# Compression layers of key and value as one set of 128-column products, and one transposition of the compressed probabilities per four heads

## The chip, the cores and the metric

The kernel runs on one core of one Trainium2 chip. The metric is device time in microseconds of one execution, lower is better. The core has five engines that run their own queues of instructions and wait for one another by semaphores: TensorE (PE; its weight loads are shown as PEld), VectorE (DVE), ScalarE (ACT), GpSimd (POOL) and SyncE (SP), which issues most of the DMAs.

## What is computed

Two layers of a decoder trunk on 256 tokens of width 1024: a recurrent block with its MLP, then native sparse attention with its MLP, and a final norm. The change lies in the attention layer. There each of four key/value groups has a compressed branch: blocks of 32 tokens (15 of them, 16 tokens apart) are flattened, a positional table is added, and a two-layer network with GELU makes one compressed key and one compressed value of each block.

```python
def _compress(z, pe, w1, w2):
    ...
    blocks = jnp.concatenate([chunks[:, r:r + nc] for r in range(CMP_RATIO)], axis=2)
    blocks = blocks + pe[None, None, :, None, :]
    flat = jnp.transpose(blocks, (0, 1, 3, 2, 4)).reshape(B, nc, G, CMP_LEN * DH)
    return jax.nn.gelu(flat @ w1, approximate=True) @ w2
...
        s_c = jnp.einsum('qghd,ngd->ghqn', qf, kc) - slopes * d_c.astype(jnp.float32)
        p_c = _masked_softmax(s_c, d_c >= 0)
        o_c = jnp.einsum('ghqn,ngd->qghd', p_c, vc)
...
        o = g[..., 0:1] * o_c + g[..., 1:2] * o_s + g[..., 2:3] * o_w
```

With 256 tokens there are only four blocks to select from, so all are selected, and the selected and the window branch are two causal attentions over 256 keys each, with keys and values of their own. The three branches are summed with sigmoid gates.

## The kernel before, in words

**Layout.** Activations are held transposed: 128 features on the partitions, 256 tokens along the row. Every large product is done in three matmuls on values split into a high and a low part (`mm3`, L307 to L310), because TensorE is fast on the split type; weights come by DMA into `raw`, ScalarE or VectorE make the high part (L316), VectorE the low one (L313). Smaller products are done in plain f32.

**Order.** The attention layer is one `Section`. Each step is added with the engines that may do it, an assumed duration, the keys it reads and writes and a wished time `t`; `Plan.emit` makes a list schedule of all steps from these and a seed, improves it by passes backwards and forwards, and issues every step in the order of the planned start. So a step that is dropped, added or given another duration may change the order of everything else on every engine, and which of ScalarE or VectorE does a step that either may do. The planner's numbers are no measured times.

**Compression.** `cproj` (L877) projects key and value for two groups each, four chunks in all; VectorE evicts each to one of three buffers `tt` (L881), and four copies, half of them by DMA (`move`, L823 to L826, on SyncE), lay its tokens into `zfs`, so that token offset and feature lie on the partitions (two offsets 16 apart times 64 features) and the block along the row: 60 blocks of four groups and two columns for the positional table, `ZW` = 62. `hidden` (L890) multiplies them with the first layer: for each of 16 offsets one product for key, whose 64 outputs go to the lower half of the partitions of PSUM bank 4, and one for value into the upper half. The 62 columns of the moving operand are followed by the GELU for both (L901 to L904). `kc_out` makes compressed keys (L908). `vc_out` first repeats the hidden values four times (`hv`), so that the product of L927 gives, for the four heads of a group that share them, 16 blocks each on 64 partitions; one product for each of four sets `a` of four heads, and VectorE multiplies each with a mask (L930) so that `bd[:, a]` is block-diagonal: four heads on 64 partitions, each with its own 64 output columns. The upper 64 partitions of `bd` and of the probabilities `pcs` are set to zero by GpSimd (L812, L814), since the product that uses them runs over 128 partitions.

**Attention.** `compressed(a)` (L985) does four heads at once: eight score products into bank 7 (L998), a softmax in eleven steps on VectorE (L1008 to L1020, one step of them on ScalarE), which leaves `cq`, 128 queries on the partitions and (half of the queries, head, block) along the row; two transpositions, one per half of the queries (L1035), into 64 partitions of bank 7, and an eviction to `pcs[a % 2]` by ScalarE (L1037). The heads' other two branches go through `scores` (L1058, L1059, with maximum on VectorE, L1065, and exponential on ScalarE, L1068), `rescale` (VectorE L1088 or ScalarE L1087), and `transposes` (L1099). `pv(j)` (L1104) then sums two heads' three branches in bank 7: first the compressed one (L1110, from `pcs` and `bd`, 256 queries at once), then the other two from `pT` and `vv`. Two heads' outputs go to the two halves of the partitions. Bank 7 is used by all of these in turn, and also by `vc_out`. Between these steps TensorE does the remaining query and key projections and, from the middle on, the first half of the output projection.

Of the kernel before, what the change touches and what calls it, by code (L numbers as in the profile page):

```python
# [68 lines left out]
EXTRA = [("gate", i) for i in range(4)] + [("w1k", 0), ("w1v", 0)]  # L69
# [150 lines left out]
def trunk_kernel(ctx: ExitStack, tc: tile.TileContext, x_in, vec_in, const_in, w2_in, wts, out):  # L220
# [557 lines left out]
    with ExitStack() as ph:  # L778
# [9 lines left out]
        bd = at.tile([P, 4, 4, 64], F32, name="bd")  # L788
# [16 lines left out]
        pcs = many([P, S], F32, "pc", 2)  # L805
# [58 lines left out]
        zfs = [zv(ptt, i * ZW * 16) for i in range(2)]  # L864
        zpt = [("pt", i, qc, b) for i in range(NPT) for qc in range(2) for b in range(2)]
        cb = pre.tile([P, 2], F32, name="cb")
        hid = pre.tile([P, 4, NCP], F32, name="hid")
        hv = pre.tile([P, 4, 2, 2, NCP], F32, name="hv")[64:]
# [21 lines left out]
        def hidden(b, t):  # L890
            hp = zview("hp", b, lambda x: x[:, :ZW])
            keys = [("zf", i, g, j) for i in range(2) for g in range(4) for j in range(2)]
            keys += [("zf", i, x) for i in range(2) for x in "pz"]
            for q_ in range(4):
                def run(e, q_=q_):
                    for l in range(4 * q_, 4 * q_ + 4):
                        for i in range(2):
                            e.matmul(hp()[own_(i)], w1[i][:, l * 64:(l + 1) * 64], zfs[i][:, :, l], start=l == 0, stop=l == 15)
                add("pe", 0.86, run, r=[("w1", i) for i in range(2)] + keys + zpt, w=[("ps", b)], t=t + 0.9 * q_)
            t += 3.6  # L900
            add("dve", 0.07, lambda e: e.tensor_copy(cb, hp()[:, 60:62]), r=[("ps", b)], w=["cb"], t=t)  # L901
            add("act", 0.2, lambda e: e.activation(hid[:, :, :NB], hp()[:, :60].rearrange("p (g n) -> p g n", g=4),
                                                   AF.Gelu_apprx_tanh, bias=cb[:, 0:1]),
                r=[("ps", b), "cb", "tab"], w=["hid"], t=t)  # L904

        def kc_out(t):
            o = zview("kco", 6, lambda x: x[:, :4 * NCP])
            add("pe", 0.3, lambda e: e.matmul(o(), w2raw[:64], hid[:64].rearrange("p g n -> p (g n)"), start=True, stop=True),  # L908
                r=["hid"], w=[("ps", 6)], t=t)
            o4 = lambda: o().rearrange("p (g n) -> p g n", g=4)  # L910
            add("act", 0.1, lambda e: e.copy(kc[:, :, 0], o4()), r=[("ps", 6), "kc0"], w=["kch"], t=t)
            for hf in range(2):
                own = own_(hf)
                add("dve", 0.15, lambda e, own=own, hf=hf: e.tensor_tensor(
                    kc[own, hf::2, 1], o4()[own, hf::2], kc[own, hf::2, 0].bitcast(F32), op=OP.subtract),
                    r=[("ps", 6), "kch", "kc0"], w=[("kcl", hf)], t=t)

        def vc_out(t):
            for g in range(4):
                dst = hv[:, g // 2 * 2:g // 2 * 2 + 2, :, g % 2].rearrange("p a b n -> p (a b) n")  # L920
                add([("act", 0.2, 0.0), ("dve", 0.15, 0.0)], copy(dst, hvs[:, g, None, :].to_broadcast([64, 4, NCP])),
                    r=["hid"], w=[("hv", g)], t=t)
            o = zview("vco", 7, lambda x: x[:64, :4 * 64].rearrange("p (a e) -> p a e", a=4))

            def run(e):
                for a in range(4):
                    e.matmul(o()[:, a], hv[:, a].rearrange("p b f n -> p (b f n)"), w2raw[64:, :64], start=True, stop=True)  # L927
            add("pe", 0.9, run, r=[("hv", g) for g in range(4)], w=[("ps", 7)], t=t)
            for a in range(4):
                add("dve", 0.34, lambda e, a=a: e.tensor_tensor(  # L930
                    bd[:64, a], o()[:, a, None, :].to_broadcast([64, 4, 64]),
                    cst[:64, C_BM:C_BM + 4, None].to_broadcast([64, 4, 64]), op=OP.mult), r=[("ps", 7)], w=[("bd", a)], t=t)
# [52 lines left out]
        def compressed(a, t, dt):  # L985
# [45 lines left out]
            ct_ = zview(("ct", a), 7, lambda x: x[:64, :S])  # L1031

            def tr(e):
                for qc in range(2):
                    e.transpose(ct_()[:, qc * P:(qc + 1) * P], sq_[:, qc].rearrange("p j n -> p (j n)"), identf)  # L1035
# [68 lines left out]
        def pv(j, t):  # L1104
# [4 lines left out]
            def run(e):  # L1109
                two = lambda c0, w, y, **k: [e.matmul(o()[own_(hf), c0:], w(hf), y(hf), **k) for hf in range(2)]  # L1110
                two(0, lambda hf: bd[:, a, j % 2 * 2 + hf], lambda hf: pcs[a % 2], start=True, stop=False)
# [4 lines left out]
            add("pe", 1.92, run, r=[("pT", n0 + i) for i in range(4)] + [("bd", a), "bd0", ("pc", a % 2), ("pc0", a % 2)] +  # L1116
# [95 lines left out]
def _arrange(inp):  # L1212
# [28 lines left out]
    w1 = {"w1k": f["nsa_w1_k"][0], "w1v": f["nsa_w1_v"][0]}  # L1241

    def piece(name, i):
# [16 lines left out]
        if name in w1:  # L1260
            w = w1[name].reshape(2, 16, 64, 64)
            return w.transpose(0, 2, 1, 3).reshape(P, -1)
# [21 lines left out]
    bm = np.where(np.arange(P)[:, None] // NCP % 4 == np.arange(8)[None, :], 1.0, 0.0)  # L1284
# [28 lines left out]
```

## Time and profile before

| what | value |
|---|---|
| median of 3 runs | 579.18 us (578.52 to 579.38) |
| the profiled execution | 579.59 us |
| its span, first to last instruction | 577.8 us |
| mean granted clock of TensorE | 0.994 |
| hidden layer's products on TensorE (L898) | 280.61 to 285.0 us |
| first compressed scores (L998) | 309.5 us |
| last weighted sum (L1110) | ends at about 383.1 us |

In the profile, times are in microseconds from the first instruction. A row of the timeline gives start, length, engine, line, operation, what is written from what, the shape of the written or loaded tile, and after an x how many equal ones follow each other. Matmuls are pipelined, so a row of several is as long as from the first start to the last end, and the step between two starts is the price of one. In brackets stands the idle time ahead and what ended it.

### The profile page before, as it was taken

The numbers are of one execution on the slowest core, as the hardware profiler recorded it, in microseconds if no ns is written. First come the engines' busy times: TensorE is split into PE (matmuls) and PEld (weight loads), VectorE is DVE, ScalarE is ACT, GpSimd is POOL, SyncE is SP. The second block draws the span as 40 slices with busy tenths as digits, with TensorE's granted clock in tenths as the row PEclk, the third lists the DMA queues.
The fourth block names the chain that finished last, engine by engine and source line by source line (L and its number), as shares of the span: only waits on it lengthen the run. The fifth ranks groups of instructions, "written<-read, shape, count | busy, mean of one in ns | idle before, by whom it ended". The sixth has DMA issues, their size and how long they took to land.

```text
span 577.8 us, 12305 instructions
## 1 busy us (share of the span) xinstructions
PE 566.2 (98%) x4878; PEld 554.0 (96%) x4878; DVE 409.5 (71%) x840; ACT 337.7 (58%) x655; POOL 46.8 (8%) x59
## 2 busy tenths in 40 slices
PE   8999999999999999999999999999999999999994
PEld 7999999999999999999999888999999999999993
DVE  6999998667765654656759999979676775553522
ACT  7699575755663533535447988865766564443400
POOL 1210000000000211312000000000000000222310
PEclk9999999999999999999999999999999999999997
DMA  8934666655656565566673253234655666466302
GB/s 296 387 120 142 206 216 204 214 184 195 203 187 219 180 201 204 177 200 242 188 246 115 70 160 101 89 110 138 199 200 195 187 199 236 152 213 219 111 1 73
DMA packets 32377, 103.66 MB, mean 179 GB/s; under 512 B 4016, under 2 KB 7216, under 8 KB 32320
## 3 DMA queue, kind: packets, MB, share of 16 engines
q1 hardware_dynamic: 31712, 102.29, 53.4%
q8 instruction: 38, 0.62, 0.4%
q10 hardware_dynamic: 576, 0.53, 0.3%
q14 instruction: 19, 0.16, 0.1%
q0 software_dynamic: 32, 0.07, 0.0%
HBM read 99.23 MB, written 1.05 MB: 174 GB/s over the span
## 4 chain that ended last, share of the span: by engine, by line
PE 85%; DVE 8%; DMA 4%; ACT 2%; issue 1%; SPq 0%; DVEq 0%
PE bank L308 25%; PE bank L309 25%; PE bank L310 25%; PE bank L1110 3%; PE bank L1099 2%; DVE wlo L313 2%; DVE xb L628 2%; DMA pt<-tt 1%; PE bank L1058 1%; DMA raw<-in_dram 1%; DMA xt<-in_dram 1%; PE bank L1059 1%; ACT whi L316 1%; PE bank L948 1%; PE bank L949 1%
## 5 line engine op out<-in xcount | busy, mean ns | idle before, releaser
L308 PE MATMUL bank<-hhl,whi 128*128 128x256 f32 x768 | 214.7, 280 | 1.2 <-DVE whi L316 1.2
L310 PE MATMUL bank<-hhl,wlo 128*128 128x256 f32 x768 | 212.6, 277 | 0.5 <-DVE wlo L313 0.5
L309 PE MATMUL bank<-hhl,whi 128*128 128x256 f32 x768 | 212.6, 277 | 0.1
L308 PEld LDWEIGHTS bank<-hhl,whi 128*128 128x128 f32 x768 | 144.2, 188 | 1.8 <-ACT x L545 1.3
L277 DVE TENSOR_TENSOR wlo<-raw,whi 128x1024 fp32r<-128x1024 f32 x115 | 143.7, 1270 | 2.3 <-ACT whi L268 2.3
L310 PEld LDWEIGHTS bank<-hhl,wlo 128*128 128x128 f32 x768 | 144.2, 188 | 0.9 <-DVE wlo L313 0.9
L309 PEld LDWEIGHTS bank<-hhl,whi 128*128 128x128 f32 x768 | 144.3, 188 | 0.6 <-DVE hhl L541 0.3
L308 PE MATMUL bank<-uhl,whi 128*128 128x256 f32 x512 | 141.5, 276 | 0.0
L309 PE MATMUL bank<-uhl,whi 128*128 128x256 f32 x512 | 141.4, 276 | 0.0
L310 PE MATMUL bank<-uhl,wlo 128*128 128x256 f32 x512 | 141.4, 276 | 0.0
L268 ACT CAST whi<-raw 128x1024 fp32r<-128x1024 f32 x116 | 118.0, 1039 | 23.1 <-issue 18.8
L308 PEld LDWEIGHTS bank<-uhl,whi 128*128 128x128 f32 x512 | 96.1, 188 | 0.0
L309 PEld LDWEIGHTS bank<-uhl,whi 128*128 128x128 f32 x512 | 96.1, 188 | 0.0
L310 PEld LDWEIGHTS bank<-uhl,wlo 128*128 128x128 f32 x512 | 96.1, 188 | 0.0
L313 DVE TENSOR_TENSOR wlo<-raw,whi 128x1024 fp32r<-128x1024 f32 (+2 forms) x74 | 79.4, 1094 | 6.8 <-ACT whi L316 6.6
L491 DVE TENSOR_TENSOR xt<-xt,bank 128x256 f32<-128x256 f32 x40 | 16.3, 418 | 86.4 <-PE bank L310 86.3
L316 ACT CAST whi<-raw 128x1024 fp32r<-128x1024 f32 (+2 forms) x64 | 61.3, 968 | 19.9 <-PE bank L309 5.4
L743 ACT ACTIVATE u<-t 128x256 f32<-128x256 f32 x64 | 26.7, 417 | 59.7 <-DVE t L738 58.7
L738 DVE SCALAR_TENSOR_TENSOR t<-bank,rstd 128x256 f32<-128x256 f32 x64 | 27.0, 424 | 46.8 <-PE bank L310 46.8
L1193 ACT ACTIVATE xg<-xt,vec 128x256 f32<-128x256 f32 x8 | 4.1, 511 | 48.0 <-DVE xt L491 48.0
L1068 ACT ACTIVATE pt<-pt,mx 128x128 f32<-128x128 f32 (+1 forms) x64 | 28.6, 448 | 4.2 <-DVE mx L1065 4.0
L461 POOL TENSOR_TENSOR acc<-xt 128x256 f32<-128x256 f32 x2 | 3.1, 1526 | 345.4 <-DVE xt L491 345.4
(182 smaller groups left out, 745.8 us busy)
## 6 DMA issues: line engine op xcount, KB each, us to landing
raw<-in_dram SPq DMA_DIRECT2D x173, 512.0 KB, 3.7
raw<-in_dram SPq DMA_DIRECT2D x4, 560.0 KB, 4.1
gw<-in_dram SPq DMA_DIRECT2D x4, 512.0 KB, 8.5
raw<-in_dram SPq DMA_DIRECT2D x6, 256.0 KB, 5.6
xt<-in_dram SPq DMA_DIRECT2D x4, 256.0 KB, 5.3
w<-in_dram SPq DMA_DIRECT2D x2, 512.0 KB, 5.5
kh<-kh SPq DMA_DIRECT2D x8, 64.0 KB, 2.8
kl<-tl SPq DMA_DIRECT2D x8, 64.0 KB, 2.5
```

The lines of the kernel that those rows point to most:

```text
L268: (act.copy if eng is None else eng.tensor_copy)(hi_t[i % NSPL][:, :n], raw_t[i % NRAW][:, :n])
L277: (eng or dve).tensor_tensor(lo[:, :n], raw_t[i % NRAW][:, :n], hi[:, :n].bitcast(F32), op=OP.subtract)
L308: pe.matmul(ps, wh, xh, start=start, stop=False)
L309: pe.matmul(ps, wh, xl, start=False, stop=False)
L310: pe.matmul(ps, wl, xh, start=False, stop=stop)
L313: return lambda e: e.tensor_tensor(o, a, h.bitcast(F32), op=OP.subtract)
L316: return lambda e: (e.copy if e is act else e.tensor_copy)(o, a)
L491: dve.tensor_tensor(xt[:, m], xt[:, m], z, op=OP.add)
L738: dve.scalar_tensor_tensor(t, z, 0.0, rs, op0=OP.max, op1=OP.mult)
L743: act.activation(u, t, AF.Square)
L1068: add("act", (0.39, 0.49)[qc], lambda e, row=row, j=j: e.activation(row, row, AF.Exp, bias=mx[:, j:j + 1], scale=-1.0, accum_out=sm[:, j:j ...
L1110: two = lambda c0, w, y, **k: [e.matmul(o()[own_(hf), c0:], w(hf), y(hf), **k) for hf in range(2)]
```

## The change

- **Hidden layer.** The first-layer weights of key and value are stored side by side on the host, so that one weight holds 128 columns: 64 for key, 64 for value. One product per offset, 16 instead of 32, multiplies it with the columns of both key and value (124). It yields four quarters, of which two are used: key's weights with key's columns, and value's with value's. The two DMA pieces `w1` keep their size, but the first now holds offsets 0 to 7 of both and the second offsets 8 to 15. Bias copy and GELU become two steps each, of 64 partitions.
- **Compressed values.** `hv` is laid out so that two products of 128 columns, one for each half `p` of the groups, replace four of 64; `bd` becomes 128 partitions with eight (half of the queries, head) of 64 columns; two masks of 512 columns replace four of 256.
- **Probabilities.** `cq` is transposed once, as 128x128, with (half of the queries, head, block) on the partitions, and evicted as 128x128 by ScalarE or VectorE. In `pv` each half of the queries then has its own block-diagonal columns: two products of 128 columns per head instead of one of 256.
- **No more zeros.** The three memsets on GpSimd go.

```diff
-EXTRA = [("gate", i) for i in range(4)] + [("w1k", 0), ("w1v", 0)]
+EXTRA = [("gate", i) for i in range(4)] + [("w1", 0), ("w1", 1)]
...
-        bd = at.tile([P, 4, 4, 64], F32, name="bd")
+        bd = at.tile([P, 2, 8, 64], F32, name="bd")
...
-        add("pool", 0.9, lambda e: e.memset(bd[64:], 0.0), w=["bd0"], t=-8)
-        for i in range(2):
-            add("pool", 0.3, lambda e, i=i: e.memset(pcs[i][64:], 0.0), w=[("pc0", i)], t=-8)
...
                     for l in range(4 * q_, 4 * q_ + 4):
-                        for i in range(2):
-                            e.matmul(hp()[own_(i)], w1[i][:, l * 64:(l + 1) * 64], zfs[i][:, :, l], start=l == 0, stop=l == 15)
-                add("pe", 0.86, run, r=[("w1", i) for i in range(2)] + keys + zpt, w=[("ps", b)], t=t + 0.9 * q_)
+                        e.matmul(hp(), w1[l // 8][:, l % 8 * P:(l % 8 + 1) * P], zall[:, :, l], start=l == 0, stop=l == 15)
+                add("pe", 0.89, run, r=[("w1", i) for i in range(2)] + keys + zpt, w=[("ps", b)], t=t + 0.9 * q_)
...
-                for a in range(4):
-                    e.matmul(o()[:, a], hv[:, a].rearrange("p b f n -> p (b f n)"), w2raw[64:, :64], start=True, stop=True)
-            add("pe", 0.9, run, r=[("hv", g) for g in range(4)], w=[("ps", 7)], t=t)
-            for a in range(4):
-                add("dve", 0.34, lambda e, a=a: e.tensor_tensor(
...
+                for p in range(2):
+                    e.matmul(o()[:, p], hv[:, p].rearrange("p b f n -> p (b f n)"), w2raw[64:, :64], start=True, stop=True)
+            add("pe", 0.45, run, r=[("hv", g) for g in range(4)], w=[("ps", 7)], t=t)
+            for p in range(2):
+                add("dve", 0.6, lambda e, p=p: e.tensor_tensor(
...
-                for qc in range(2):
-                    e.transpose(ct_()[:, qc * P:(qc + 1) * P], sq_[:, qc].rearrange("p j n -> p (j n)"), identf)
-            add("pe", 0.22, tr, r=[qk], w=b7, t=t)
-            add("act", 0.26, lambda e: e.copy(pc[:64], ct_()), r=b7, w=[pk], t=t)
+            add("pe", 0.11, lambda e: e.transpose(ct_(), sq_.rearrange("p q j n -> p (q j n)"), identf), r=[qk], w=b7, t=t)
+            add([("act", 0.3, 0.0), ("dve", 0.2, 0.15)], lambda e: copy(pc, ct_())(e), r=b7, w=[pk], t=t)
...
-                two(0, lambda hf: bd[:, a, j % 2 * 2 + hf], lambda hf: pcs[a % 2], start=True, stop=False)
+                for qc in range(2):
+                    cut = o()[:, qc * P:(qc + 1) * P]
+                    for hf in range(2):
+                        e.matmul(cut[own_(hf)], bd[:, p, qc * 4 + j % 2 * 2 + hf], pcs[a % 2], start=qc == 0, stop=False)
```

The new steps also give the planner other durations, so the order changes from the hidden layer on. Three places on TensorE matter below. The line numbers of the changed kernel are a little lower (L895 is the old L898, L1032 the old L1035, L1054 the old L1058, L1095 the old L1099).

First the hidden layer (`pt` holds the laid-out columns, `w` the weights), the value projection behind it (L948 to L950), key's output (L908) and value's (L927). Before:

```order
L310 MATMUL bank_3445<-hhl,wlo_92 128x256
L898 MATMUL bank_3477<-pt,w_3240 64x62
L898 MATMUL bank_3477<-pt,w_3241 64x62
...
L948 MATMUL bank_3522<-whi_86,hhl 128x304
...
L908 MATMUL bank_3543<-hid,w2raw 128x64
L927 MATMUL bank_3545<-w2raw,hv 64x64 x4
L948 MATMUL bank_3554<-whi_86,hhl 128x304
```

and now:

```order
L310 MATMUL bank_3434<-hhl,wlo_92 128x256
L895 MATMUL bank_3472<-pt,w_3240 128x124 x8
L895 MATMUL bank_3472<-pt,w_3241 128x124 x8
L948 MATMUL bank_3501<-whi_86,hhl 128x304
...
L908 MATMUL bank_3524<-hid,w2raw 128x64
L948 MATMUL bank_3528<-whi_86,hhl 128x304
...
L927 MATMUL bank_3538<-w2raw,hv 128x64 x2
L948 MATMUL bank_3528<-whi_86,hhl 128x304
```

The 32 products have become 16. Twelve value products stand between the hidden layer and key's output as before; value's output, which followed at once, now comes six value products later.

Second, the first scores: `sa_3213` and `sb_3217` hold the first query chunk, `sa_3214` the second. Before:

```order
L1059 MATMUL bank_3766<-kl,sb_3217 128x256
L308 MATMUL bank_3731<-hhl,whi_85 128x256
...
L1058 MATMUL bank_3781<-kh,sb_3217 128x512
L1059 MATMUL bank_3781<-kl,sb_3217 128x512
L1058 MATMUL bank_3788<-kh,sa_3214 128x256
```

and now:

```order
L1055 MATMUL bank_3744<-kl,sb_3217 128x256
L308 MATMUL bank_3710<-hhl,whi_85 128x256
...
L308 MATMUL bank_3758<-hhl,whi_86 128x256
...
L1054 MATMUL bank_3769<-kh,sb_3217 128x512
L1055 MATMUL bank_3769<-kl,sb_3217 128x512
L1054 MATMUL bank_3775<-kh,sa_3214 128x256
```

Six products stood ahead of the 512-column scores; now there are twelve, the last six of another projection.

Third, from the last compressed score of the first four heads (L998) to their transposition (`cst,cq`). Before:

```order
L998 MATMUL bank_3796<-kc,sb_3218 128x32 x2
L308 MATMUL bank_3811<-hhl,whi_86 128x256
...
L1099 MATMUL bank_3833<-cst,pt 128x128 x3
L1099 MATMUL bank_3840<-cst,pt 128x128 x3
L1058 MATMUL bank_3846<-kh,sb_3218 128x512
...
L1058 MATMUL bank_3864<-kh,sb_3218 128x256
...
L1099 MATMUL bank_3879<-cst,pt 128x128 x3
L1099 MATMUL bank_3885<-cst,pt 128x128 x3
L308 MATMUL bank_3893<-hhl,whi_87 128x256
...
L1035 MATMUL bank_3914<-cst,cq_3260 64x128 x2
```

and now:

```order
L998 MATMUL bank_3785<-kc,sb_3218 128x32 x2
L308 MATMUL bank_3758<-hhl,whi_86 128x256
...
L1054 MATMUL bank_3810<-kh,sb_3218 128x256
L1055 MATMUL bank_3810<-kl,sb_3218 128x256
L1095 MATMUL bank_3816<-cst,pt 128x128 x3
L1095 MATMUL bank_3822<-cst,pt 128x128 x3
...
L308 MATMUL bank_3850<-hhl,whi_87 128x256
...
L1095 MATMUL bank_3862<-cst,pt 128x128 x3
L1095 MATMUL bank_3868<-cst,pt 128x128 x3
L1032 MATMUL bank_3876<-cst,cq_3260 128x128
```

Before, 36 products (L308 to L310), 12 transpositions, two 512-column and two 256-column score products stood between them. Now it is 24 products, 12 transpositions and the two of 256 columns; the two 512-column ones and 12 products come after the transposition. On VectorE the same stretch, from L1008 to L1020, has 12 rows of other heads' work among its own ten instead of 14. Over the whole section five of the rescaling steps (L1088) go from VectorE to ScalarE, and one of the four evictions of `pcs` goes to VectorE.

On SyncE the eight DMAs of the compression (`pt<-tt`) stand in the same order behind the same loads as before.

More of the change, by code (lines that the diff above doesn't have):

```diff
@@ L804, in trunk_kernel @@
         w1 = many([P, 1024], F32, "w1", 2)
-        pcs = many([P, S], F32, "pc", 2)
+        pcs = many([P, P], F32, "pc", 2)
         for i in range(2):
@@ L896, in run @@
                     for l in range(4 * q_, 4 * q_ + 4):
-                        for i in range(2):
-                            e.matmul(hp()[own_(i)], w1[i][:, l * 64:(l + 1) * 64], zfs[i][:, :, l], start=l == 0, stop=l == 15)
-                add("pe", 0.86, run, r=[("w1", i) for i in range(2)] + keys + zpt, w=[("ps", b)], t=t + 0.9 * q_)
+                        e.matmul(hp(), w1[l // 8][:, l % 8 * P:(l % 8 + 1) * P], zall[:, :, l], start=l == 0, stop=l == 15)
+                add("pe", 0.89, run, r=[("w1", i) for i in range(2)] + keys + zpt, w=[("ps", b)], t=t + 0.9 * q_)
             t += 3.6
[L901 to L904, printed above, removed]
+            for i in range(2):
+                own, c = own_(i), i * ZW
+                add("dve", 0.1, lambda e, own=own, c=c: e.tensor_copy(cb[own], hp()[own, c + 60:c + 62]), r=[("ps", b)],
+                    w=[("cb", i)], t=t)
+                add("act", 0.25, lambda e, own=own, c=c: e.activation(
+                    hid[own, :, :NB], hp()[own, c:c + 60].rearrange("p (g n) -> p g n", g=4), AF.Gelu_apprx_tanh,
+                    bias=cb[own, 0:1]), r=[("ps", b), ("cb", i), "hid", "tab"], w=[("hid", i)], t=t)
         def kc_out(t):
@@ L1115, in run @@
                     two(P, lambda hf: vv[:, 1, b, 2 * p + hf], lambda hf: y(hf)[:, S:], start=False, stop=b == 1)
-            add("pe", 1.92, run, r=[("pT", n0 + i) for i in range(4)] + [("bd", a), "bd0", ("pc", a % 2), ("pc0", a % 2)] +
+            add("pe", 1.92, run, r=[("pT", n0 + i) for i in range(4)] + [("bd", p), ("pc", a % 2)] +
                 [("v", h, b) for h in range(2) for b in range(2)], w=bk, t=t)
@@ L1240, in _arrange @@
     wo = wo[perm]
-    w1 = {"w1k": f["nsa_w1_k"][0], "w1v": f["nsa_w1_v"][0]}
+    w1 = [f["nsa_w1_%s" % n][0].reshape(2, 16, 64, 64).transpose(0, 2, 1, 3).reshape(P, 16, 64) for n in "kv"]
+    w1 = np.concatenate(w1, axis=2)
     def piece(name, i):
@@ L1259, in piece @@
             return wv[2 * i:2 * i + 2].transpose(1, 0, 2).reshape(P, -1)
-        if name in w1:
-            w = w1[name].reshape(2, 16, 64, 64)
-            return w.transpose(0, 2, 1, 3).reshape(P, -1)
+        if name == "w1":
+            return w1[:, i * 8:i * 8 + 8].reshape(P, -1)
         if name == "q":
@@ L1283, in _arrange @@
         mc.append(np.where(ok, 1.0, 0.0))
-    bm = np.where(np.arange(P)[:, None] // NCP % 4 == np.arange(8)[None, :], 1.0, 0.0)
+    bm = np.where(np.arange(P)[:, None] // NCP == np.arange(8)[None, :], 1.0, 0.0)
     qs = np.zeros((P, 8))
```

20 lines of the change are left out of this document (10 added, 10 removed).

## The prediction

> **What bounds the kernel now.** I read the page first, then TensorE's waits, then the busy time by stretch over the attention section (263 to 402 us), then the timeline where the change lies. The page:
>
> ```profile
> span 577.8 us, 12305 instructions
> PE 566.2 (98%) x4878; PEld 554.0 (96%) x4878; DVE 409.5 (71%) x840; ACT 337.7 (58%) x655; POOL 46.8 (8%) x59
> ```
>
> TensorE is busy throughout. That holds in the changed section too, where VectorE comes close behind it (two of the stretches; the columns are the stretch, its length, then PE, PEld, DVE, ACT, POOL):
>
> ```profile
> 310.00:320.00 10.00, 10.00 (x88) 9.13 (x89) 9.58 (x48) 9.35 (x32) 0.00 (x0) 1.00 0.07 16
> 350.00:360.00 10.00, 10.00 (x88) 8.10 (x87) 9.77 (x41) 9.04 (x31) 0.00 (x0) 1.00 0.17 33
> ```
>
> Of TensorE's waits, two lie in this section, both on short copies by DMA:
>
> ```profile
> PE bank L898 <- DMA pt<-tt: 0.3, 1, 0.3
> PE bank L1058 <- DMA sa<-tl: 0.2, 1, 0.2
> ```
>
> So a microsecond is gained or lost here only where TensorE's own steps get shorter or longer, or where its new order meets a wait. Memsets taken off GpSimd, evictions by ScalarE or VectorE, and their smaller counterparts cost nothing by themselves, while TensorE has other products to do.
>
> **Hidden layer.** TensorE's timeline around it, and, from the groups by line, L898 itself and the one f32 product with a full 128-column weight and many repeats (L648):
>
> ```profile
> 280.40 0.28 PE L310 MATMUL bank<-hhl,wlo 128*128 128x256 f32 x1
> 280.61 0.41 PE L898 MATMUL bank<-pt,w 128*64 128x62 f32 x2
> 281.37 3.65 PE L898 MATMUL bank<-pt,w 128*64 128x62 f32 x62 [0.35 <-DMA pt<-tt]
> 284.94 0.41 PE L948 MATMUL bank<-whi,hhl 128*128 128x304 f32 x1
> 285.19 0.30 PE L949 MATMUL bank<-wlo,hhl 128*128 128x304 f32 x1
> 285.33 0.30 PE L950 MATMUL bank<-whi,hhl 128*128 128x304 f32 x1
> L898 PE MATMUL bank<-pt,w 128*64 128x62 f32 x64 | 4.1, 287 | 0.3 <-DMA pt<-tt 0.3
> L648 PE MATMUL bank<-xb,gw 128*128 128x256 f32 x64 | 14.1, 379 | 0.0
> ```
>
> The code has 32 products of 64 columns; the chip shows 64, each f32 product being two instructions. From 281.37 to 284.94 there are 62: 0.058 us each, 0.115 per pair of halves. The change leaves 32 instructions with 124 moving columns. L648 takes 14.1 / 64 = 0.22 us for 256 columns; half of it is 0.11. So 32 x 0.11 = 3.5 us instead of 64 x 0.058 = 3.7, from the same DMA on: the last one starts at 281.37 + 31 x 0.11 = 284.78. What is really saved is the passage into the next product. The last L898 starts at 281.37 + 3.65 - 0.29 = 284.73; L948 comes 0.21 after it and L949 0.25 after L948, where the step is otherwise 0.14 (285.19 to 285.33). A full-width f32 group should leave as the transposition of the next part does: 0.23 from its last instruction to the second product after it, here 0.03 more for the 304 columns. L949 comes at about 285.04 instead of 285.19: **-0.15 us** (between -0.3 and, if each instruction cost a whole 0.22, +3.5).
>
> The Trainium skill's "TensorEngine Tiling (Array Packing)", Theoretical Speedup, gives column tiles of up to 64 columns up to twice the throughput, which speaks against this change: the two old halves would run at once. Its "TensorE: Matmul & The Clock Gate", LDWEIGHTS (loading the stationary operand), prices a weight load by its columns, P / 1.2 ns, which makes an estimated 53 ns for 64 and 107 for 128, hence no difference; the trace's 0.058 per half agrees with this second rule, not the first. By the first alone the sum would be an estimated 1.7 us worse.
>
> **Transposition.** Two old ones at the first four heads, with the products around them, and three ordinary transpositions after:
>
> ```profile
> 316.39 0.28 PE L309 MATMUL bank<-hhl,whi 128*128 128x256 f32 x1
> 316.50 0.28 PE L310 MATMUL bank<-hhl,wlo 128*128 128x256 f32 x1
> 316.62 0.38 PE L1035 MATMUL bank<-cst,cq 128*64 128x128 f32 x2
> 316.76 0.37 PE L308 MATMUL bank<-hhl,whi 128*128 128x256 f32 x1
> 316.96 0.29 PE L309 MATMUL bank<-hhl,whi 128*128 128x256 f32 x1
> 317.56 0.49 PE L1099 MATMUL bank<-cst,pt 128*128 128x128 f32 x3
> ```
>
> The second L1035 starts at 316.62 + 0.11 = 316.73 (two end after 0.38, three of L1099 after 0.49: one more adds 0.11), 0.23 before L309. From L310 at 316.50 to L309 at 316.96 pass 0.46 us, in which L310 and L308 are 2 x 0.115 (316.39 to 316.50 is 0.11): the pair costs 0.23. A full-width one costs no more than a 64-column one by the same 0.11, so one goes away at each of four places. 4 x 0.11: **-0.43 us**, all on the path. The eviction of 128x128 instead of 64x256 lies beside products.
>
> **Weighted sums.** One of the eight groups of probabilities times values:
>
> ```profile
> 357.19 0.65 PE L1110 MATMUL bank<-pc,bd 128*64 128x256 f32 x4
> 357.68 1.47 PE L1110 MATMUL bank<-pT,vv 128*64 128x256 f32 x16
> 359.08 0.51 PE L1058 MATMUL bank<-kh,sa 128*128 128x512 f32 x1
> ```
>
> The four bd instructions, two pairs, take 0.49 until 357.68, of which I count 0.05 as entry: 0.22 a pair. The 16 that follow are four pairs of 256 and four of 128 columns; of the 1.40 until 359.08, 0.88 are the long ones and about 0.1 the exit, so a short pair takes about 0.11. The change makes four short pairs of two long ones: 0.44 either way. I add 0.01 for each of eight groups: **+0.1 us** (0 to +0.2).
>
> **Outputs of the compression.**
>
> ```profile
> 286.46 0.28 PE L950 MATMUL bank<-whi,hhl 128*128 128x256 f32 x1
> 286.74 0.43 PE L908 MATMUL bank<-hid,w2raw 64*128 64x64 f32 x2
> 287.98 0.30 PE L949 MATMUL bank<-wlo,hhl 128*128 128x304 f32 x1
> ```
>
> From 286.46 to 287.98 pass 1.52 us, of which about 0.26 are two products: the visit costs 1.26. Four f32 products become two of double width, but a new entry and exit come in, since six value products now stand between key's and value's output. An entry was at most 0.16 (286.46 to 286.74, less 0.12); an exit like the one after the hidden layer's some 0.2. I take **0** (-0.3 to +0.3). The Trainium skill, "TensorEngine Tiling (Array Packing)", Key Properties, says that a change of tiling mode drains TensorE; by it the hidden layer loses two drains and this place gains one. The 0.21 before L898 and L948 agree.
>
> **The new order.** Two waits move. First, the scores of the second query chunk:
>
> ```profile
> 308.15 0.40 PE L1059 MATMUL bank<-kl,sb 128*128 128x512 f32 x1
> 308.71 0.36 PE L1058 MATMUL bank<-kh,sa 128*128 128x256 f32 x1 [0.16 <-DMA sa<-tl]
> 309.25 0.40 PE L1059 MATMUL bank<-kl,sa 128*128 128x512 f32 x1
> 309.49 0.29 PE L998 MATMUL bank<-kc,sa 128*128 128x32 f32 x2
> ```
>
> A 512-column step is 0.24 (309.25 to 309.49); here it is 0.56. TensorE lost 0.32 us until the copy landed. The new order puts 12 products ahead instead of 6, and 6 x 0.115 = 0.69 covers that: **-0.3 us** (0 to -0.32). What is late next is the second point: TensorE may now come to the first compressed transposition too soon.
>
> ```profile
> 310.07 0.37 PE L998 MATMUL bank<-kc,sb 128*128 128x32 f32 x2
> L1008 DVE TENSOR_TENSOR cs<-bank,cst x4: 284/288/291, 311.0 to 362.1; 128x128 f32<-128x128 f32 x4
> L1020 DVE TENSOR_TENSOR cq<-cs,cm x4: 286/292/293, 315.4 to 366.4; 128x128 f32<-128x128 f32 x4
> L1065 DVE CUSTOM_DVE_ANT_0 pt<-bank,cst 128x256 f32<-128x256 f32 x32 | 12.8, 417 | 0.5 <-PE bank L1059 0.4
> L1088 DVE TENSOR_SCALAR pt<-pt,sm 128x256 f32<-128x256 f32 x27 | 9.1, 349 | 0.1
> L1088 DVE TENSOR_SCALAR pt<-pt,sm 128x128 f32<-128x128 f32 x24 | 6.4, 282 | 0.1
> L1078 DVE SCALAR_TENSOR_TENSOR sm<-sm,gts 128x4 f32<-128x4 f32 x16 | 2.5, 157 | 0.4 <-ACT pt L1068 0.2
> L313 DVE TENSOR_TENSOR tl<-tt,kh 128x256 fp32r<-128x256 f32 x4 | 1.7, 422 | 0.1
> ```
>
> VectorE's chain for the first four heads runs from 311.0 to 315.4 + 0.29 = 315.7, 4.7 us; it began about 0.5 after the compressed scores (310.07 + 0.37 = 310.44). In the new order this stretch of VectorE drops a maximum pass of 256, a scale and a split of 256 and adds two rescales, one of each width: 349 + 282 - 417 - 157 - 422 = -365 ns, so 4.35 us. With 0.26 for the scores to land, 0.1 to 0.5 to begin and about 0.2 to hand over, TensorE can transpose 4.9 to 5.3 us after its last compressed score starts. The work that stands between now is 24 products (2.76), two 256-column scores (0.24) and 12 transpositions (1.32): 4.3, with 0.3 for the score itself and passages 4.6. Before, it was 36 products, 12 transpositions and four scores, 6.2, and nothing waited. **+0.4 us** (0 to +0.7) while TensorE waits; behind the waiting transposition stand the next scores and products, which VectorE needs in turn. At the second place 5.5 us of work stand before the transposition instead of 5.8, at the third 4.5 instead of 5.5 (but with a shorter VectorE chain), at the fourth 7.1 instead of 6.2.
>
> **Sum.** -0.15 - 0.43 + 0.1 + 0 - 0.3 + 0.4 = -0.38 us against the profiled execution (579.59 us, of which 577.8 are span), which lies 0.4 above the median of the three runs (579.18). I put the change on the median: **578.8 us**, -0.07%. A measurement of this kernel can tell about 0.2% (1.16 us) from no change, so this would read as the same. The bounds of the terms, without the hidden layer's far one, give -1.8 to +1.0; unlikely to meet all at one end, so 577.9 to 579.9 for this case alone.
>
> **Rivals.**
> - *The compressed chain becomes the bound (slower).* Where the four heads' softmax still takes VectorE the 4.7 to 5.0 us that it took, the cover decides: it pays as soon as the chain plus 1.0 us (0.26 + 0.5 + 0.2) is longer than the work between. First place 5.7 against 4.6, third 5.7 against 4.9, second 6.0 against 5.9: 1.1 + 0.8 + 0.1 = 2.0, in place of my 0.4. That gives 578.8 + 1.6 = 580.4, and more if late evictions follow. For it: VectorE at 9.58 and 9.77 of 10 in these stretches. Against: five rescales move from VectorE to ScalarE in the new order. Chance 0.17.
> - *Both DMA waits go and the transposition does not wait (faster).* The hidden layer's wait hangs on a chain: the fourth compression chunk reuses the first one's buffer and waited for its copy,
>
> ```profile
> 278.26 0.42 DVE L881 TENSOR_TENSOR tt<-bank,rstd 128x256 f32<-128x256 f32 x1 [2.88 <-DMA pt<-tt]
> ```
>
>  then its own copy had to land at 281.3, while the fillers ended at 280.61. If these copies land 0.7 sooner, that and the 0.4 go: 578.8 - 1.1 = 577.7. Against: SyncE issues the same eight copies in the same order behind the same weights. Chance 0.18.
> - *Full width doesn't hide its weight loads (slower).* Were each of the 32 instructions to cost L648's whole 0.22, the hidden layer takes 3.5 us more: 582.3. A smaller loss of the same kind comes if old pairs of halves did run at once and 0.058 was what a pair costs: 32 x (0.11 - 0.058) = 1.7 more, 580.5. The Trainium skill's Theoretical Speedup, named above, would lead there; the 0.115 per pair speaks against it. Against the larger one: L648 hides 128-column loads under 256 columns, and three transpositions hide theirs under 128. Chance 0.05.
>
> **How the numbers follow.** The forecast has 0.60. Faster by over 0.2% comes from the second rival, 0.18, and 0.02 from the forecast's lower end; slower from the first and third, 0.17 + 0.05, less 0.02 that stays within. Hence 0.20, 0.60, 0.20. The range reaches to both rivals next to the forecast: 577.4 to 580.7.
>
> **What would show it.** Right: 32 instructions in the hidden layer 0.11 apart, still behind a DMA; four transpositions of full width; no 0.32 gap before the second chunk's scores; a gap of some tenths before the first compressed transposition. Wrong: hidden instructions 0.2 apart, gaps over 0.7 us before the compressed transpositions, or new waits of TensorE on rescaled rows or weights that the before does not show.

## The result and the profile after

The changed kernel takes **582.56 us** (median of 6 runs, 581.58 to 583.02) against 579.55 (578.52 to 580.06, 6 runs) before: a ratio of 1.0051 (95% interval 1.004 to 1.0061), slower by 3.0 us, where 578.8 was forecast. The profiled execution took 582.47 us, of which the span is 580.7 (577.8 before), at a mean granted clock of 0.996. The page and the group of the hidden layer (L895, formerly L898):

```profile
span 580.7 us, 12289 instructions
PE 569.4 (98%) x4870; PEld 559.0 (96%) x4870; DVE 408.2 (70%) x834; ACT 339.5 (58%) x661; POOL 45.4 (8%) x56
L895 PE MATMUL bank<-pt,w 128*128 128x124 f32 x32 | 7.0, 389 | 0.8 <-DVE tt L843 0.8
```

TensorE has 8 instructions fewer and is busy 3.2 us longer. One of the 32 instructions now lasts 389 ns on average; one of the old 64 lasted 287. The timeline of TensorE around them:

```profile
280.87 0.28 PE L310 MATMUL bank<-hhl,wlo 128*128 128x256 f32 x1
281.95 6.98 PE L895 MATMUL bank<-pt,w 128*128 128x124 f32 x32 [0.81 <-DVE tt L843]
288.59 0.48 PE L948 MATMUL bank<-whi,hhl 128*128 128x304 f32 x1
288.91 0.30 PE L949 MATMUL bank<-wlo,hhl 128*128 128x304 f32 x1
```

The 32 take 6.64 us until 288.59, a step of 0.211 where 0.11 was forecast; 62 of the old ones took 3.57. From the start of the row to the second product after it (L949) pass 6.96 us instead of 3.82: +3.14, as much as the whole loss. The wait ahead is still there. VectorE's L843, named as its end, was done at 280.72, so it was another: the last copy `pt<-tt` lands at 281.40 in the trace, and TensorE's queue takes the six semaphores for this line from 280.8 to 281.8. e9_after_later_hidden below removes the wait by planning the copies later.

The outputs of the compression, now two visits with six value products between them:

```profile
290.19 0.28 PE L950 MATMUL bank<-whi,hhl 128*128 128x256 f32 x1
290.40 0.43 PE L908 MATMUL bank<-hid,w2raw 64*128 64x64 f32 x2
...
291.00 0.30 PE L949 MATMUL bank<-wlo,hhl 128*128 128x304 f32 x1
...
291.51 0.28 PE L950 MATMUL bank<-whi,hhl 128*128 128x256 f32 x1
291.72 0.66 PE L927 MATMUL bank<-w2raw,hv 64*128 64x64 f32 x4
...
292.55 0.30 PE L949 MATMUL bank<-wlo,hhl 128*128 128x304 f32 x1
```

From L950 to L949 are 0.81 and 1.04 us; less 0.26 for the two ordinary products in each, the visits cost 0.55 + 0.78 = 1.33 instead of 1.26. The transposition (L1032), at the first four heads and at the second, and one weighted sum (L1110 and L1106):

```profile
318.29 0.82 PE L1095 MATMUL bank<-cst,pt 128*128 128x128 f32 x6
319.17 0.33 PE L1032 MATMUL bank<-cst,cq 128*128 128x128 f32 x1
...
335.84 0.39 PE L1055 MATMUL bank<-kl,sb 128*128 128x512 f32 x1
336.07 0.27 PE L1032 MATMUL bank<-cst,cq 128*128 128x128 f32 x1
336.10 0.37 PE L308 MATMUL bank<-hhl,whi 128*128 128x256 f32 x1
336.31 0.29 PE L309 MATMUL bank<-hhl,whi 128*128 128x256 f32 x1
...
360.36 0.66 PE L1110 MATMUL bank<-pc,bd 128*64 128x128 f32 x8
360.84 1.03 PE L1106 MATMUL bank<-pT,vv 128*64 128x256 f32 x9
...
362.24 0.39 PE L308 MATMUL bank<-oh,whi 128*128 128x256 f32 x1
```

At the second place 0.47 us pass from L1055 to L309, of which L1055 is 0.24 and L308 0.115: one transposition costs 0.115, the pair cost 0.23. At the first, six transpositions would have released TensorE at 318.29 + 6 x 0.11 = 318.95; L1032 came at 319.17, 0.2 late. The sum takes 362.24 - 360.36 = 1.88 us, as before. VectorE in the first of these stretches:

```profile
310.00:320.00 10.00, 9.93 (x76) 9.04 (x75) 9.76 (x52) 8.12 (x32) 0.00 (x0) 1.00 0.33 110
```

It is 9.76 of 10 busy, yet TensorE stays at 9.93: VectorE did not become the bound.

### The profile page after: what moved, and what is told of

The parts are those of the page before. It is cut to its first block, busy times and chain, and to the rows that moved or that the text cites. A ratio compares the mean times of both kernels' runs of the same rounds, so it can differ in the third digit from the quotient of the medians.

```text
span 580.7 us, 12289 instructions
## 1 busy us (share of the span) xinstructions
PE 569.4 (98%) x4870; PEld 559.0 (96%) x4870; DVE 408.2 (70%) x834; ACT 339.5 (58%) x661; POOL 45.4 (8%) x56
## 4 chain that ended last, share of the span: by engine, by line
PE 87%; DVE 9%; DMA 1%; issue 1%; ACT 0%; DVEq 0%; SPq 0%
PE bank L308 26%; PE bank L310 25%; PE bank L309 25%; DVE wlo L313 2%; PE bank L1106 2%; PE bank L1095 2%; DVE xb L628 2%; PE bank L895 1%; PE bank L1110 1%; PE bank L1054 1%; DMA pt<-tt 1%; PE bank L948 1%; PE bank L1055 1%; PE bank L949 1%; PE bank L950 1%
## 5 line engine op out<-in xcount | busy, mean ns | idle before, releaser
L308 PE MATMUL bank<-hhl,whi 128*128 128x256 f32 x768 | 214.8, 280 | 1.0 <-DVE whi L316 1.0
L310 PE MATMUL bank<-hhl,wlo 128*128 128x256 f32 x768 | 213.1, 278 | 0.2 <-DVE wlo L313 0.2
L309 PE MATMUL bank<-hhl,whi 128*128 128x256 f32 x768 | 213.0, 277 | 0.0
L308 PEld LDWEIGHTS bank<-hhl,whi 128*128 128x128 f32 x768 | 144.9, 189 | 1.6 <-ACT x L545 1.2
L310 PEld LDWEIGHTS bank<-hhl,wlo 128*128 128x128 f32 x768 | 144.8, 189 | 0.6 <-DVE wlo L313 0.6
L309 PEld LDWEIGHTS bank<-hhl,whi 128*128 128x128 f32 x768 | 144.9, 189 | 0.1
L308 PE MATMUL bank<-uhl,whi 128*128 128x256 f32 x512 | 141.5, 276 | 0.0
L309 PE MATMUL bank<-uhl,whi 128*128 128x256 f32 x512 | 141.4, 276 | 0.0
L310 PE MATMUL bank<-uhl,wlo 128*128 128x256 f32 x512 | 141.4, 276 | 0.0
L308 PEld LDWEIGHTS bank<-uhl,whi 128*128 128x128 f32 x512 | 96.1, 188 | 0.0
L309 PEld LDWEIGHTS bank<-uhl,whi 128*128 128x128 f32 x512 | 96.1, 188 | 0.0
L310 PEld LDWEIGHTS bank<-uhl,wlo 128*128 128x128 f32 x512 | 96.1, 188 | 0.0
L1064 ACT ACTIVATE pt<-pt,mx 128x256 f32<-128x256 f32 (+1 forms) x64 | 28.6, 448 | 3.2 <-DVE mx L1061 2.8
```

The costliest lines, as they stand in the source:

```text
L308: pe.matmul(ps, wh, xh, start=start, stop=False)
L309: pe.matmul(ps, wh, xl, start=False, stop=False)
L310: pe.matmul(ps, wl, xh, start=False, stop=stop)
L1064: add("act", (0.39, 0.49)[qc], lambda e, row=row, j=j: e.activation(row, row, AF.Exp, bias=mx[:, j:j + 1], scale=-1.0, accum_out=sm[:, j:j ...
```

## The experiments

Three theories were open. **A**: a moving operand whose columns lie 16 f32 apart streams at half rate, and before, the two halves of a pair ran at once, which hid that. **B**: a weight load of 128 columns does not hide under 124 streamed ones. **C**: a full-width f32 load takes 0.2 us here. Each ratio is against the kernel before on the same chip, with its 95% interval.

**Adjacent columns.**

```diff
-e.matmul(hp(), w1[l // 8][...], zall[:, :, l], ...)
+e.matmul(hp(), w1[l // 8][...], ptt[:, l * 124:(l + 1) * 124], ...)
```

> The changed kernel, but each hidden product streams 124 adjacent columns of the tile instead of 124 columns that lie 16 apart; it multiplies other numbers, so the compressed branch is not the reference's. Theory A (the strided moving operand streams at half rate, and the old pairs of halves ran at once): the 32 instructions of the hidden layer step 0.107 to 0.11 us instead of 0.211, the layer takes 3.5 instead of 6.75 us, and the kernel 579.3 (579.0 to 579.7). Theory B (a weight load of 128 columns does not hide under 124 streamed ones) and theory C (a full-width f32 load here takes 0.2 by itself): still 0.21 a step, and 582.5 for the kernel.

```profile
281.26 3.73 PE L895 MATMUL bank<-pt,w 128*128 128x124 f32 x32
284.75 0.39 PE L948 MATMUL bank<-whi,hhl 128*128 128x304 f32 x1
```

3.49 us for 32, a step of 0.109; 578.86 us, ratio 0.9982 (0.9973 to 0.9991), a little below A's bounds. Weights, loads, widths, count and TensorE's order are those of the changed kernel, only the place of the columns differs. B and C fall. The place also decides which copies an instruction needs: the first ones read less of the tile and start 0.11 us after the last projection (281.15) instead of 1.08. So of the 3.7 us that the kernel gains, 3.24 are the layer's (284.98 - 281.26 = 3.72 until L949, instead of 6.96); this wait is part of the rest.

**Which distance is free.** One run with four groups of eight with the columns 16, 8, 4 and 2 f32 apart (L897, L899, L901, L903).

```diff
+e.matmul(hp(), w, ptt[:, l:l + 8 * 124:8], **k)
```

> The changed kernel with the hidden layer's four groups of eight instructions streaming 124 columns that lie 16, 8, 4 and 2 f32 apart in turn (other numbers than the reference's, but the same count and width). Theory A: 0.21 a step at 16; at 2 the contiguous 0.107; between them one place where it jumps, at 4 or at 8, and no value in between if a line of 16 bytes is what counts. Theories B and C: 0.21 in all four groups, since load and column count do not change.

```profile
281.35 1.91 PE L897 MATMUL bank<-pt,w 128*128 128x124 f32 x8 [0.66 <-DVE tt L843]
283.08 1.99 PE L899 MATMUL bank<-pt,w 128*128 128x124 f32 x8
284.89 1.94 PE L901 MATMUL bank<-pt,w 128*128 128x124 f32 x8
286.66 1.08 PE L903 MATMUL bank<-pt,w 128*128 128x124 f32 x8
287.49 0.39 PE L956 MATMUL bank<-whi,hhl 128*128 128x304 f32 x1
```

Eight take 1.73, 1.81, 1.77 and 0.83 us: 0.22 a step at 16, 8 and 4, and 0.104 at 2 (0.11 between most of the single starts, as for e1's adjacent columns). The jump lies between 2 and 4, as A allowed.

**Distance 3, and fewer columns.** One run with eight each of 124 columns 3 f32 apart (L897), then 93, 62 and 31 columns 16 apart (L899, L901, L903), at full width.

```diff
+e.matmul(hp(), w, ptt[:, l:l + 3 * 124:3], **k)
...
+e.matmul(hp()[:, :62], w, zall[:, :62, l], **k)
```

> The changed kernel with the hidden layer's four groups of eight instructions streaming in turn 124 columns 3 f32 apart, then 93, 62 and 31 columns 16 f32 apart, at full width (other numbers than the reference's). Theory A, 1.7 ns a column at stride 16 as long as the next weight load (0.107 or less) is covered: 0.158, 0.107 and then no less than a floor of about 0.107. At stride 3 (12 bytes), where in e2_strides 2 was free and 4 was not: 0.11 if it counts whether two fetches share a line of 16 bytes now and then, 0.16 to 0.2 if each fetch of a new line costs. Theory B (load and stream one after the other, 0.107 + 0.83 ns a column): 0.21, 0.184, 0.158, 0.133.

```profile
281.11 1.50 PE L897 MATMUL bank<-pt,w 128*128 128x124 f32 x8
282.44 1.45 PE L899 MATMUL bank<-pt,w 128*128 128x93 f32 x8
283.71 1.05 PE L901 MATMUL bank<-pt,w 128*128 128x62 f32 x8
284.58 1.02 PE L903 MATMUL bank<-pt,w 128*128 128x31 f32 x8
285.43 0.39 PE L956 MATMUL bank<-whi,hhl 128*128 128x304 f32 x1
```

Steps of 0.166, 0.159, 0.109 and 0.106. So the price is 1.7 ns a column (0.211 / 124, 0.159 / 93, 0.109 / 62) until a floor is met: 31 columns still take 0.106 (0.112 between most of the single starts, as e1's 124 adjacent ones). B's series (0.184, 0.158, 0.133) is not seen. Distance 3 lies between 2 and 4, as expected if each fetch of a new line costs.

**Did the halves run at once?** The kernel before, its 64 half-width products unchanged but in another order, first four window positions at a time, then all of key ahead of all of value.

```diff
-for l in range(4 * q_, 4 * q_ + 4):
-    for i in range(2):
+for i in range(2):
+    for l in range(4 * q_, 4 * q_ + 4):
```

> The kernel before, with the same 64 half-width products of the hidden layer in another order only: in each group of four window positions first key's four, then value's four, instead of in turn. Theory A (a pair of halves ran at once, each half streaming 62 strided columns in 0.11): most neighbours now use the same half and run one after the other, so 64 instructions take 64 x 0.105 = 6.7 us, less 0.1 for each of the 7 places where the halves meet: 5.9 to 6.8 us instead of 3.57. Serial theory, the prediction's own (0.058 for each half, whatever its neighbour): 3.5 to 3.7 us.

```profile
281.89 4.23 PE L898 MATMUL bank<-pt,w 128*64 128x62 f32 x64
286.05 0.40 PE L948 MATMUL bank<-whi,hhl 128*128 128x304 f32 x1
```

4.16 us, which neither theory gave. Between single starts, TensorE's records show 0.107 for the first three steps and the last four before the exit, and two instructions per 0.107 nearly all the way between: an instruction is paired with one of the other half that stands some places off in the program. One run, 580.73 us. The larger distance decides:

```diff
+for i in (q_ // 2,):
+    for l in range(q_ % 2 * 8, q_ % 2 * 8 + 8):
```

> The kernel before, with all 32 instructions of key's half of the hidden layer first and then all 32 of value's (the same 64, another order; e3_halves_apart had them four window positions at a time and took 4.16 us, between what the two theories gave). Theory A (neighbours of the same half run one after the other at 0.107, of different halves at once), with what e3 showed, that TensorE pairs an instruction with one of the other half some 4 to 8 places further on: 64 x 0.107 = 6.8, less 4 to 8 pairs of 0.107 where the halves meet: 6.0 to 6.5 us, and the kernel takes 579.6 + 2.5 = 582.1 (581.8 to 582.6). Serial theory (0.058 for each half whatever its neighbour, and e3's excess from something else): 3.6 to 4.2 us, 579.6 to 580.2.

```profile
281.28 6.64 PE L898 MATMUL bank<-pt,w 128*64 128x62 f32 x64
287.85 0.41 PE L948 MATMUL bank<-whi,hhl 128*128 128x304 f32 x1
```

6.57 us for the same 64 instructions, 582.4 us and a ratio of 1.0056 (1.0038 to 1.0074). The records show 0.107 a step, with four pairs where the halves meet. So one half of 62 columns costs 0.107, and 0.115 bought two of them. The serial reading, 0.058 for each half, falls.

**One part alone, and the rest alone.** First the hidden layer of the change in the kernel before, then the change with the old hidden layer.

```diff
-EXTRA = ... + [("w1k", 0), ("w1v", 0)]
+EXTRA = ... + [("w1", 0), ("w1", 1)]
...
+e.matmul(hp(), w1[l // 8][...], zall[:, :, l], ...)
```

> The kernel before with the hidden layer alone changed to full width (weights' layout, two bias copies and two activations with it); transposition, weighted sums and value's output as before. Theory A: 32 instructions step 0.211 us, 6.7 us instead of 3.57, and the kernel takes 579.6 + 3.1 = 582.7 (582.2 to 583.2): more than the whole change costs, since the saved transpositions are missing. If the loss needed the rest of the change as well (a wait that only the new order brings): 579.6 to 581.

583.09 us, ratio 1.0057 (1.0044 to 1.0071): the hidden layer alone costs 3.3 us. In the profiled execution the granted clock happened to fall in the middle of it (columns: the stretch, its length, PE busy and instructions, clock, DMA share, GB/s; the first row is e5's, the second the same stretch of the changed kernel):

```profile
284.64:288.06 3.42, 3.42 (x18) 0.50 0.51 123
284.64:288.06 3.42, 3.42 (x18) 1.00 0.94 262
```

Eighteen instructions are under way in this stretch at a clock of 0.50, as many as at 1.00, and the single starts lie 0.210 to 0.214 us apart in both. At half the clock the strided stream costs the same, so the array's clock is not what it waits for; that it is the reading of the tile fits with e2 and e6.

Now the whole change, but the old hidden layer.

```diff
-EXTRA = ... + [("w1", 0), ("w1", 1)]
+EXTRA = ... + [("w1k", 0), ("w1v", 0)]
...
+for i in range(2):
+    e.matmul(hp()[own_(i)], w1[i][...], zfs[i][:, :, l], ...)
```

> The changed kernel with the hidden layer alone put back to pairs of 64-column products, its weights' layout with it; transposition, weighted sums and value's output as changed. If the hidden layer is the whole loss (theories A, B and C alike): its 64 instructions step 0.115 a pair again, 3.6 us, and the kernel takes 582.56 - 3.1 = 579.4 (579.0 to 579.8). If the compressed chain on VectorE became the bound (the prediction's first rival): 581 to 582.5. Prediction's other terms (-0.43 transposition, +0.1 sums, -0.3 and +0.4 waits): 579.55 - 0.2 = 579.3.

578.26 us, ratio 0.9981 (0.9971 to 0.9991): 1.1 to 1.4 us faster than before, and lower than any theory said. The rest of the change is a gain. Part of what was not foreseen shows where the compression's outputs pass:

```profile
286.34 0.28 PE L947 MATMUL bank<-whi,hhl 128*128 128x256 f32 x1
...
287.38 0.30 PE L946 MATMUL bank<-wlo,hhl 128*128 128x304 f32 x1
```

In this order key's and value's products stand together and start at once (L905 at 286.55, L924 at 286.56; before, value's started 0.42 after key's): 1.04 - 0.26 = 0.78 us instead of 1.26, 0.48 gained that the changed kernel's two visits do not have.

**Can full width and its order be mended?** First only the wait: the planner is told that the copies between halves land after 3.4 us, not 2.0.

```diff
-add("sp", 0.6, ..., r=r, w=w, t=t, lag=2.0)
+add("sp", 0.6, ..., r=r, w=w, t=t, lag=3.4)
```

> The changed kernel with one number of the planner altered: the compression's copies between halves count 3.4 us to their landing (the trace's median) instead of 2.0, so that more products are queued ahead of the hidden layer. Theory A: the wait of 1.1 us before the hidden layer goes, its 32 instructions still step 0.211, and the kernel takes 582.56 - 0.9 = 581.7 (581.2 to 582.2). If that wait, and not the step, were the loss: 579.5 to 580.

```profile
283.49 0.28 PE L952 MATMUL bank<-whi,hhl 128*128 128x256 f32 x1
283.61 6.92 PE L897 MATMUL bank<-pt,w 128*128 128x124 f32 x32
290.18 0.48 PE L950 MATMUL bank<-whi,hhl 128*128 128x304 f32 x1
```

581.44 us, ratio 1.0033 (1.0023 to 1.0044). The wait is gone from TensorE's list, the layer still takes 6.58 us: the wait was about 1 us of the changed kernel's time (before had most of it too), and the step is untouched by it. Then a layout in which the 16 columns of a window position are adjacent in each group: VectorE's eviction writes its rows in that order, and the bias column takes the unused sixteenth place.

```diff
+xp = x.rearrange("p (l n) -> p n l", l=16)
+add("dve", 0.34, lambda e: e.tensor_tensor(xp, zp(), rp, op=OP.mult), ...)
...
+zc = ptt[:, :8 * 256].rearrange("p (b l n) -> p b l n", l=16, n=16)
+e.matmul(hp()..., w1[l // 8][...], zc[:, :, l], ...)
```

> The changed kernel with the reference's numbers, the tile laid out so that the columns of one window position are adjacent (runs of 16 f32; VectorE writes the projection's rows in that order, and the bias column goes into a free slot). Theory A: 32 instructions of 128 columns step 0.11, 3.5 us, and the kernel takes 582.56 - 3.2 = 579.0 (578.5 to 579.5), if the strided write costs VectorE no more than 0.3 us on the path of the last copy. Theories B and C: 582.5.

```profile
L898 PE MATMUL bank<-pt,w 128*128 128x128 f32 x32 | 3.8, 277 | 0.8 <-DVE tl L313 0.8
```

277 ns instead of 389 for an instruction, though it has four columns more, and 3.57 us for the 32 (281.70 to 285.27); 578.15 us, ratio 0.9981 (0.9972 to 0.999), below what A gave. With the copies planned later:

> e7_dense_full_width with the same number altered. Steps of 0.112 as there, and the wait of 1.1 us before the hidden layer gone: 578.15 - 0.9 = 577.3 (576.8 to 577.9). If what is gained there comes back as a wait further on (VectorE's splits of the values' weights, or the scores): 578.1.

577.24 us, ratio 0.9958 (0.9945 to 0.9971), as forecast. That the number fits is in part chance: from e7's trace to this one the wait gets 1.0 us shorter and the outputs, which now start at once, another 0.47, so about half a microsecond is lost at places that were not traced.

**Half width on adjacent columns.** The same layout with e4's pairs (`zc[:, 4 * i:4 * i + 4, l]` for half `i`).

> e4_pairs_in_after (pairs of 64-column halves, the rest as changed) with the dense layout of e7_dense_full_width. Theory A: each half streams 64 adjacent columns in 0.054 and the two halves run at once, so a pair steps between 0.054 (streams bound) and 0.11 (the two loads of 64 columns come one after the other): 1.8 to 3.5 us for the layer and 576.6 to 578.3 for the kernel, against 578.26 for e4_pairs_in_after. If the stride had nothing to do with the pairs' 0.115: 3.6 us and 578.3.

```profile
281.25 2.05 PE L899 MATMUL bank<-pt,w 128*64 128x64 f32 x62 [0.28 <-DMA pt<-tt]
283.23 0.41 PE L950 MATMUL bank<-whi,hhl 128*128 128x304 f32 x1
```

62 instructions in 1.98 us: 0.064 a pair (0.058 between most starts), A's lower end. Yet the kernel takes 579.24 us, ratio 0.9996 (0.9986 to 1.0006), no gain. The timeline of VectorE, ScalarE and TensorE behind the layer, and the clock:

```profile
283.52 2.35 DVE L313 TENSOR_TENSOR wlo<-raw,whi 128x1024 fp32r<-128x1024 f32 x2
...
285.79 0.15 DVE L903 COPY cb<-bank 128x1 f32<-128x1 f32 x1
286.04 0.31 ACT L904 ACTIVATE hid<-bank,cb 128x60 f32<-128x60 f32 x1 [1.43 <-DVE cb L903]
...
286.40 0.43 PE L910 MATMUL bank<-hid,w2raw 64*128 64x64 f32 x2 [1.35 <-ACT hid L904]
```

```profile
284.28:287.69 3.41, 2.06 (x16) 1.00 0.66 141
287.69:291.11 3.42, 3.42 (x17) 0.50 0.84 322
```

The layer is now done before the plan expects it; the bias copy stands behind two weight splits on VectorE, TensorE waits 1.35 us, and then the granted clock is at half for 3.42 us. By the clock that is 1.7 us lost; the products show 1.5: the 16 steps from 287.52 on take 3.59 us, the same ones in e4 2.05. The mean clocks of the other runs, 0.990 to 0.994 against e11's 0.993 to 0.996 below, suggest that it was not this execution alone. The next run gives the plan the true durations:

```diff
-add("pe", 0.86, run, ...)
+add("pe", 0.47, run, ...)
...
-add("sp", 0.6, ..., r=r, w=w, t=t, lag=2.0)
+add("sp", 0.6, ..., r=r, w=w, t=t, lag=3.4)
```

> e8_dense_pairs with the same number altered and the hidden layer's duration in the plan set to what was measured (0.47 us for 16 instructions, not 0.86). In e8 the pairs stepped 0.058, but TensorE waited 0.5 us before them and 1.3 us behind them for the activation (its bias copy stood behind two splits of 1.2 us on VectorE), and the granted clock then fell to 0.5 for some 3.4 us (1.7 us lost). If the waits are what brings the fall of the clock: neither appears, and the kernel takes 579.24 - 0.5 - 1.3 - 1.7 = 575.7 (575.5 to 577.3). If the clock falls because of the pairs themselves: the clock falls again behind the layer, and 577.3 to 578.5.

```profile
284.87 2.08 PE L901 MATMUL bank<-pt,w 128*64 128x64 f32 x64
286.89 0.41 PE L952 MATMUL bank<-whi,hhl 128*128 128x304 f32 x1
```

```profile
284.00:286.00 2.00, 2.00 (x46) 1.00 0.98 356
286.00:288.00 2.00, 2.00 (x42) 1.00 1.06 299
```

2.02 us for 64, no wait, the clock at 1.00, and **576.47 us**, ratio 0.9934 (0.992 to 0.9948): the fastest kernel of this study, 0.8 above the forecast and within its range. So pairs at this pace do not bring the fall of the clock by themselves; it came where the waits stood. That a wait is enough is not shown: e5's clock fell behind one of 0.94 us, but behind those of 0.81 and 0.83 in the changed kernel and in e7 it did not.

## Why the prediction was wrong

**The hidden layer (-0.15 forecast, +3.14 measured)** is the step that failed, at "L648 takes 14.1 / 64 = 0.22 us for 256 columns; half of it is 0.11". L648 streams adjacent columns, `zall[:, :, l]` streams columns 16 f32 apart. e1_contiguous shows 0.109 for the one and the changed kernel 0.211 for the other, with the same weights, widths and count. The trace of before held the warning: one L898 lasted 287 ns for 62 columns, and one of L1110's products of the same width less, 273 ns, for 128 adjacent ones:

```profile
L1110 PE MATMUL bank<-pT,vv 128*64 128x128 f32 x64 | 6.2, 273 | 0.0
```

e11's group has L898's instruction with 64 adjacent columns, 224 ns.

The second failure stands beside the first: "0.058 us each, 0.115 per pair of halves" took a step between starts for the price of a half. e12_key_then_value shows 0.107 for a half by itself; before, two ran in that time. So the stride is not the whole loss: in either layout one full-width instruction takes nearly twice as long as the pair that it replaces (0.211 against 0.115 at 16 apart, 0.109 against 0.063 adjacent), as it streams both halves' columns one after the other; adjacent columns make both cheaper. The prediction took the 0.058 as proof against the rule on column tiles (the Trainium skill, "TensorEngine Tiling (Array Packing)", Theoretical Speedup: up to twice the throughput for at most 64 columns). The runs agree with that rule: the halves run two at a time where they stand in turn (64 in e12's order take 6.57 us), and on adjacent columns e11's pairs step 0.063 (2.02 / 32) against e1's 0.109 for one instruction of full width. The price by columns that it preferred ("TensorE: Matmul & The Clock Gate", LDWEIGHTS) agrees too, with the floor of 0.106 to 0.112 in e6_widths, but that floor binds only where the stream is shorter. A rule that would have foreseen the stride was not weighed: the Trainium skill's "SBUF — State Buffer" (the note on 16-byte lines in the section on the DMA port swizzle) says that full rate needs at least two fetches from each line of 16 bytes. e2_strides agrees at 2 f32 (two in a line, 0.104) and at 4 and more (one, 0.22). Counted in such lines, 124 columns lie in 93 of them at 3 apart and in 124 at 4 apart, and both cost 1.8 ns a line (0.166 / 93 and 0.22 / 124). Where the same note calls four f32 of stride free, the measured 0.22 decides against it.

**The third rival** ("full width doesn't hide its weight loads", 582.3, chance 0.05) had the size right and the cause wrong: e1's loads hide under adjacent columns, and e6's steps follow the columns. Its smaller form, the halves at once, was true but gave 1.7 us, because it too priced 124 columns at 0.11.

**The transposition (-0.43)** held: 0.115 instead of 0.23 at each of four places. **The weighted sums (+0.1)** cost 0: 1.88 us as before, four short pairs and their entry in 0.48. **The outputs (0)** cost 0.07 as two visits, within the bounds; as one visit they would have gained 0.48 (e4). **The wait for the query's copy (-0.3)** went, it is not among TensorE's waits any more (in e4's order one of 0.7 us for such a copy comes back at a later head). **The first compressed transposition (+0.4)** waited 0.2. **The hidden layer's DMA wait**, taken as unchanged, grew a little: from the last projection to the first instruction of the run pass 281.95 - 280.87 = 1.08 us, and 281.37 - 280.40 = 0.97 before, in which two instructions had found place. e2 has 0.93 with the changed kernel's order, so 0.1 is no more than executions differ by.

Together 3.14 - 0.46 + 0.07 - 0.3 + 0.2 + 0.1 = 2.75, against 2.9 between the two spans. That these lie so close is in part chance: 0.47 of the 2.9 had arisen ahead of the hidden layer's wait, where the last projection starts at 280.87 instead of 280.40 (e2, in the same order, at 280.42). From there to the end it is 2.43, so some 0.3 us were gained at places that were not traced. The other terms came out near their forecasts, and one term missed by 3.3 us. The first two rivals did not come: VectorE's chain made TensorE wait 0.2 us, and both DMA waits did not go together. e4 puts the other parts of the change by themselves at -1.1 us (0.0019 x 579.7) instead of the sum's -0.23; 0.48 of it is the single visit, and 0.33 that its hidden layer did not wait (4.46 us from the last projection to the second value product, 4.79 before). The rest was not traced to single rows and stays open, since the plan reorders with every edit.

## What to carry to other kernels

Before a product's step is taken from another line of the profile, compare the access pattern of the moving operand, not only rows, columns and type: an f32 operand whose columns lie 3 or more elements apart costs 1.5 to 2 times as much here. A mean duration that is too long for its columns gives it away. And a step between starts is the price of an instruction, as the remark ahead of the profile before has it, only if its neighbours use the same part of the array; where two halves are in turn, put one half by itself to see what it costs. A shorter step pays only if the plan knows it: e8's gain of 1.6 us was lost to a wait behind it and to the clock.

## What the hardware showed unexpectedly

- Columns 2 f32 apart stream at the full rate (0.104 us for 124, adjacent ones 0.109), 3 apart at 0.166, 4 to 16 apart at 0.21 to 0.23, and at 16 apart this does not change with the granted clock (e5: 0.210 to 0.214 a step at 0.50, 0.211 at 1.00).
- Instructions on the two column halves overlap even when they do not stand next to each other: in e3 and e12 an instruction ran beside one of the other half that stood, by the four single steps at each end of e3 and the four pairs in the middle of e12, about four places off in the program; beyond that nothing overlapped.
- In e8 and in e5 the granted clock went to half for 3.42 us behind 3.41 us in which TensorE was busy for 2.06 and 2.47; with 2.64 of 3.45 ahead of the changed kernel's hidden layer it did not. The Trainium skill, "TensorE: Matmul & The Clock Gate", Part 1, names an idle window of about that length for the return to half rate. The traces agree in length, but TensorE wasn't idle for all of it.
